# A decoder layer's first gate/up block, begun with two products on half of the tokens

## The chip, the cores and the metric

The kernel runs on one core of one Trainium2 chip. The metric is the device time of one execution in microseconds (us), taken as the median of several runs; the profile is of one execution of its own.

## What is computed

One layer of a post-norm decoder: 512 tokens, model width 2048, all in fp32. In the order of the work:

1. One projection of h feeds two token mixers: grouped attention in a sliding window of 128 with sinks, and causal differential attention. Both add a relative-position bias. They are gated, mixed and projected (W_o), then h = LN1(alpha*h + ...).
2. Cross attention into 256 memory rows (W_cq, W_kv, four heads, W_co), then h = LN2(alpha*h + ...).
3. The feed-forward part, with d_ff = 5632, then LN3:

```
g, u = split(h @ w_gate_up);  h = LN3(alpha*h + (silu(g) * u) @ w_down)
```

Each LN subtracts the mean, multiplies by the inverse standard deviation, then by a gain per column, and adds a bias per column.

## The kernel before

**Matmuls.** Every fp32 product is made of three fp32r products (`mm3`, L255 to L262): xh·wh, xh·wl and xl·wh, where `split` (L165) makes the parts: ACT casts h (L168), VectorE subtracts for l (L169). Tokens lie in four blocks t of 128. Weights come in chunks of 128x1024 (512 KB) over SyncE's queue (`dma`, L175); `dma_aside` (L178) is the software queue of POOL.

**The start.** POOL writes the bias rows to DRAM (rv_d), spreads them with three big transfers into rep_d, then copies the first keys (kd, eight transfers of 128 KB) and the first queries (q) into place; attention's first scores (L458) need those.

**W_co and LN2.** `gemm_n` (L277) makes W_co's four columns of 512; after each token block's matmuls `done` (L879) adds the residual (L880) and the statistics (L712). After column 3 `moments` (L714) makes mean and inverse deviation per token block, partly on POOL. `scale` (L724) normalises each of 16 tiles of 128x512 on ACT (L731) and multiplies by the gain's row on VectorE (L732).

**The gate/up products.** w_gate_up is taken in 11 blocks g of 512 gate and 512 up columns. Rows are cut in two halves, too, so a block has four quarters (11, 12, 21, 22), each of four chunks. Its result is made of seven products instead of eight, in Strassen's manner: each is a token operand (a11, s1, s2n, s4, s3, a12, a22) times a weight operand (11, t1, t2, 22, t3, 21, t4). The token operands cover 256 tokens and half of the columns: a11 and a12 are token blocks 0 and 1, a21 and a22 blocks 2 and 3, the others sums of them. The weight operands t1, t2 and t4 are sums of quarters that VectorE makes (L978 to L985).

`token_operands` (L917) runs ahead of all products, for all four parts j: it transposes z on TensorE (L928), evicts with the bias on ACT (L929), makes the sums on VectorE (L938 to L944) and splits all seven operands. `Quarters` (L949) loads the weights' chunks into the 13 buffers of the pool rp, makes operand chunks three ahead of their use and loads ten ahead. A product is 48 matmuls, 12 for each chunk. Results go to banks x, w and y; `each` (L1028) copies or adds them.

**Orders.** Only the loop over the sevens (L1098) has TensorE's order written by hand; elsewhere the compiler of the program orders each engine. In the last block, after product 2, `hidden` (L1066) reads five blocks of finished activations back (tiles araw, two of 512 KB each, from rp), waits for 6.0 us of matmul time to be issued and transposes them (L1076) between the matmuls, in that written order. rp's buffers are handed out in the program's order. W_down then runs in blocks of 5, 5 and 1; in the first, the bias row of LN2 is added to the residual (L1138), read back from z_d.

Of the kernel before, what the change touches and what calls it, by code (L numbers as in the profile page):

```python
# [128 lines left out]
def layer_kernel(ctx, tc, x, xT, memT, table, onehot, w_in, sinks, lams, subw, w_a, w_b, w_o,  # L129
# [272 lines left out]
    lt = cp.tile([P, 256], F32, name="lt")  # L402
# [293 lines left out]
    class Norm:  # L696
# [17 lines left out]
        def moments(self, t):  # L714

            mv = small(4, f"mv{t}")
            nc.vector.bn_aggr(mv[:, 0:2], self.st[t].rearrange("p c s -> p (c s)"))
            neg = small(1, f"neg{t}")
# [42 lines left out]
    z = [[None] * 4 for _ in range(NT)]  # L761
    ln1 = Norm(0, z)
    for c in range(4):
        for t in range(NT):
            z[t][c] = at(s="z", pool=zp)
            dma_aside(z[t][c], x[cols(t), c * 512 : (c + 1) * 512])
# [100 lines left out]
    for h in range(HC):  # L867
# [3 lines left out]
        oc.append((at(F32R, "och"), at(F32R, "ocl")))  # L871
        split(*oc[h], o_ps)

    ln1.add_bias()
    ln2 = Norm(1, z)
    for c in range(4):
        ln2.row(0, c, at(s="lnrow", pool=rows_pool))

        def done(t, ps, c=c):  # L879
            nc.vector.scalar_tensor_tensor(z[t][c], z[t][c], ALPHA, ps, ALU.mult, ALU.add)  # L880
            ln2.stats(t, c)
            if c == 3:
                ln2.moments(t)

        gemm_n(W_co, c, oc, done, tail=2)

# [3 lines left out]
    rp = open_pool("rp", 13, phase)  # L890

    def rt(s):
        return rp.tile([P, 1024], F32, tag="rp", name=nm(s))

# [5 lines left out]

    zs = z_tiles()
    for c in (0, 2, 1, 3):
        for t in range(NT):
            ln2.scale(t, c, zs[t][c])
    z = zs
    side.close()
    sp = open_pool("sp", 14, phase)
    gp = open_pool("gp", 6, side, side="right")

    def st(s, dt=F32R):  # L910
        return sp.tile([P, 2048], dt, tag="sp", name=nm(s))


    OPS = ("a11", "s1", "s2n", "s4", "s3", "a12", "a22")
    s_hl = {op: [st(op).rearrange("p (k q) -> p k q", k=HK) for _ in range(2)] for op in OPS}

    def token_operands(j):  # L917

        b = ln_gb[:, 2 * ln2.i + 1, :]
        halves = []  # L920
        for half in range(2):
            raw = rt("sraw")
            r4 = raw.rearrange("p (h k q) -> p h k q", h=2, k=2)
            for i in range(2):
                k = 2 * j + i + half * HK
                tp = bank("hT")
                for t in range(NT):
                    nc.tensor.transpose(tp[:, cols(t)], z[t][k // 4][:, cols(k % 4)], ident)  # L928
                nc.scalar.activation(r4[:, :, i, :], tp.rearrange("p (h q) -> p h q", h=2),  # L929
                                     AF.Identity, bias=b[:, k : k + 1])  # L930
            halves.append([raw[:, :512], raw[:, 512:]])
        (a11, a21), (a12, a22) = halves
        x, y = rt("ssum"), rt("ssum")
        s1, s2n, s4, s3 = x[:, :512], x[:, 512:], y[:, :512], y[:, 512:]
        made = {"a11": a11, "s1": s1, "s2n": s2n, "s4": s4, "s3": s3, "a12": a12, "a22": a22}
        for op in OPS:
            if op == "s1":
                nc.vector.tensor_sub(s1, a22, a21)  # L938
            elif op == "s2n":
                nc.vector.scalar_tensor_tensor(s2n, a11, -1.0, s1, ALU.mult, ALU.subtract)  # L940
            elif op == "s4":
                nc.vector.scalar_tensor_tensor(s4, s2n, -1.0, a12, ALU.mult, ALU.subtract)
            elif op == "s3":
                nc.vector.tensor_sub(s3, a11, a21)  # L944
            v = made[op].rearrange("p (k q) -> p k q", k=2)
            split(*(x[:, 2 * j : 2 * j + 2, :] for x in s_hl[op]), v)


    class Quarters:  # L949
# [4 lines left out]

        NEED = {"11": 0, "12": 1, "22": 2, "21": 5}

        def __init__(self):
            self.loads = [(28 * g + 4 * n + c, g, q, c) for g in range(NF)
                          for q, n in self.NEED.items() for c in range(4)]
            self.raw, self.parts, self.made, self.loaded = {}, [], 0, 0  # L960

        def load_to(self, n):
            while self.loaded < len(self.loads) and self.loads[self.loaded][0] < n:
                _, g, q, c = self.loads[self.loaded]
                i = 16 * g + 4 * list(QUARTERS).index(q) + c
                self.raw[g, q, c] = t = rt("r" + q)
                dma(t, w_gu[i * P * 1024 : (i + 1) * P * 1024].rearrange("(p f) -> p f", p=P))
                self.loaded += 1

        def make_to(self, n):  # L970
            while self.made < min(n, 28 * NF):
                g, i = divmod(self.made, 28)
                op, c = self.ORDER[i // 4], i % 4
                self.load_to(self.made + 1)
                r = {q: self.raw.get((g, q, c)) for q in QUARTERS}
                if op == "t1":
                    src = wst.tile([P, 1024], F32, tag="raw", name=nm("t1"))
                    nc.vector.tensor_add(src, r["11"], r["12"])  # L978
                elif op == "t2":
                    src = r["11"]  # L980
# [254 lines left out]
```

## Time and profile before

| what | us |
|---|---|
| median of 3 runs | 2751.59 (2750.56 to 2752.66) |
| the profiled execution | 2750.57 |
| its span, first to last instruction | 2748.8 |
| TensorE busy | 2691.0 (98%) |
| VectorE busy | 1544.7 (56%) |
| ACT busy | 1002.9 (36%) |
| POOL busy | 209.9 (8%) |
| mean granted TensorE clock | 0.991 |

The profile's times count from the span's first instruction; 1.8 us of the execution lie around the span. An arrow "x<-y" reads "x made from y"; "[0.73 <-DVE neg L719]" behind a row is the idle time before it and what ended it, and "issue" there means that the profile shows no wait for anything. In a timeline neighbouring instructions of one kind are merged (x15), and the end of one overlaps the start of the next. L-numbers are lines of the kernel before.

### The profile page before, as it was taken

To read this page: it belongs to the slowest core of one execution; us is meant where nothing else is said; L and a number is where in the kernel's file an instruction comes from. 1 tells how busy PE (TensorE), PEld (TensorE's weight loads), DVE (VectorE), ACT (ScalarE), POOL (GpSimd) and SP (SyncE) were. 2 spreads that over 40 slices of the span, in tenths; PEclk is the share of its full clock that TensorE was granted. 3 is DMA by queue.
4 is the path that set the end of the run, shared out by engine and by line. 5 is a ranking of instruction groups with operands and counts; after the bars stand their busy time and mean duration, and the time that the engine had idled before them with its cause. 6 is when DMAs were issued, how large, how long until landed. Compare 5 with 4: busy or idle time off the path is not lost.

```text
span 2748.8 us, 31093 instructions
## 1 busy us (share of the span) xinstructions
PE 2691.0 (98%) x12274; PEld 2221.4 (81%) x12274; DVE 1544.7 (56%) x2023; ACT 1002.9 (36%) x1424; POOL 209.9 (8%) x366
## 2 busy tenths in 40 slices
PE   8899999999999999999879999999999999999998
PEld 6788888888888888888768888888888878888886
DVE  4456545652333343365888888777777873233227
ACT  3344433442222232154454444444444451122112
POOL 2311212000000011000100000000000010000003
PEclk9999999999999999999989999999999999999999
DMA  8644636322222245333333334333233473343332
GB/s 276 151 113 105 146 113 145 100 84 93 99 93 100 93 136 170 93 114 118 115 128 115 117 136 138 138 130 123 100 130 120 139 269 101 93 137 99 101 95 105
DMA packets 107554, 341.64 MB, mean 124 GB/s; under 512 B 15071, under 2 KB 15631, under 8 KB 107408
## 3 DMA queue, kind: packets, MB, share of 16 engines
q1 hardware_dynamic: 81872, 277.91, 30.4%
q0 software_dynamic: 25536, 61.75, 8.7%
q8 instruction: 96, 1.57, 0.2%
q14 instruction: 50, 0.41, 0.0%
HBM read 301.79 MB, written 25.74 MB: 119 GB/s over the span
## 4 chain that ended last, share of the span: by engine, by line
PE 94%; DVE 2%; DMA 2%; issue 1%; ACT 1%; POOL 0%; POOLq 0%; DVEq 0%
PE ps L261 19%; PE ps L259 19%; PE ps L257 19%; PE y L257 4%; PE y L261 4%; PE y L259 4%; PE x L259 3%; PE x L261 3%; PE x L257 3%; PE w L257 3%; PE w L261 3%; PE w L259 3%; DMA kd<-kl 1%; PE o L543 1%; PE aT L1076 1%
## 5 line engine op out<-in xcount | busy, mean ns | idle before, releaser
L169 DVE TENSOR_TENSOR wl<-raw,wh 128x1024 fp32r<-128x1024 f32 (+1 forms) x313 | 379.4, 1213 | 804.5 <-ACT wh L168 803.7
L168 ACT CAST wh<-raw 128x1024 fp32r<-128x1024 f32 (+1 forms) x313 | 326.7, 1045 | 912.7 <-PE ps L261 495.1
L168 ACT CAST wh<-r 128x1024 fp32r<-128x1024 f32 x264 | 278.4, 1055 | 389.4 <-PE y L261 204.5
L169 DVE TENSOR_TENSOR wl<-r,wh 128x1024 fp32r<-128x1024 f32 x264 | 322.0, 1221 | 168.0 <-ACT wh L168 168.0
L257 PE MATMUL ps<-xh,wh 128*128 128x512 f32 x928 | 369.7, 399 | 6.8 <-ACT wh L168 4.5
L259 PE MATMUL ps<-xl,wh 128*128 128x512 f32 x928 | 369.4, 398 | 0.9 <-DVE xl L169 0.9
L261 PE MATMUL ps<-xh,wl 128*128 128x512 f32 x928 | 368.9, 398 | 0.0
L257 PE MATMUL ps<-wh,ah 128*128 128x512 f32 x656 | 258.4, 394 | 0.0
L261 PE MATMUL ps<-wh,al 128*128 128x512 f32 x656 | 258.1, 393 | 0.0
L259 PE MATMUL ps<-wl,ah 128*128 128x512 f32 x656 | 258.0, 393 | 0.0
L257 PEld LDWEIGHTS ps<-xh,wh 128*128 128x128 f32 x928 | 175.2, 189 | 45.8 <-ACT wh L168 4.5
L259 PEld LDWEIGHTS ps<-xl,wh 128*128 128x128 f32 x928 | 175.1, 189 | 39.7 <-DVE xl L169 1.8
L261 PEld LDWEIGHTS ps<-xh,wl 128*128 128x128 f32 x928 | 175.3, 189 | 37.6
L257 PE MATMUL x<-wh,a 128*128 128x512 f32 x352 | 140.4, 399 | 10.8 <-ACT sraw L929 5.8
L259 PE MATMUL x<-wl,a 128*128 128x512 f32 x352 | 140.0, 398 | 5.2 <-DVE wl L169 5.2
L257 PEld LDWEIGHTS ps<-wh,ah 128*128 128x128 f32 x656 | 123.2, 188 | 26.8
L261 PEld LDWEIGHTS ps<-wh,al 128*128 128x128 f32 x656 | 123.2, 188 | 26.5
L259 PEld LDWEIGHTS ps<-wl,ah 128*128 128x128 f32 x656 | 123.2, 188 | 26.3
L261 PE MATMUL x<-wh,a 128*128 128x512 f32 x352 | 139.5, 396 | 0.0
L261 PE MATMUL w<-wh,s 128*128 128x512 f32 x352 | 137.5, 391 | 0.0
L257 PE MATMUL w<-wh,s 128*128 128x512 f32 x352 | 137.5, 391 | 0.0
L259 PE MATMUL w<-wl,s 128*128 128x512 f32 x352 | 137.4, 390 | 0.0
(270 smaller groups left out, 4925.7 us busy)
## 6 DMA issues: line engine op xcount, KB each, us to landing
r<-in_w_gu SPq DMA_DIRECT2D x176, 512.0 KB, 3.3
raw<-in_w_in SPq DMA_DIRECT2D x131, 512.0 KB, 3.6
raw<-in_w_down SPq DMA_DIRECT2D x88, 512.0 KB, 3.5
raw<-in_w_o SPq DMA_DIRECT2D x32, 512.0 KB, 3.5
acts_d<-g POOLq DMA_DIRECT2D x44, 256.0 KB, 2.9
araw<-acts_d SPq DMA_DIRECT2D x22, 512.0 KB, 5.0
raw<-in_w_a SPq DMA_DIRECT2D x16, 512.0 KB, 3.4
raw<-in_w_b SPq DMA_DIRECT2D x16, 512.0 KB, 3.2
```

Source lines behind the costliest of these rows:

```text
L168: nc.scalar.copy(h, src)
L169: nc.vector.tensor_sub(l, src, f32(h))
L257: nc.tensor.matmul(ps, ah, bh, start=start, stop=False, **kw)
L259: nc.tensor.matmul(ps, ah, bl, start=False, stop=False, **kw)
L261: nc.tensor.matmul(ps, al, bh, start=False, stop=stop, **kw)
L543: nc.tensor.matmul(o4[i][:, :, dst, :], v[x][:, cols(kb)], p[y][:, :, src, :], start=first and m == 0, stop=last and m == 2, skip_group_ch ...
L1076: nc.tensor.transpose(tp[:, cols(t)], raw[t // 2][:, (t % 2) * 512 + i * P :][:, :P], ident)
```

## The change

- The order of VectorE and ACT is written by hand from W_co's last column to the first block's third product, and TensorE's from W_co's last column to the end of the sevens.
- The first block g = 0 has another order of products: 11 and 21 first. Both read only token blocks 0 and 1 (a11, a12) and add into the same bank x. `first_half(c)`, c = 0 to 7, makes their operands; the other five operands are made by functions that stand behind the matmuls of chunks 4 to 19 (list `after`), and the normalisation of the blocks stands in between.
- LN2's 16 tiles are normalised in place, without gain: two on ACT, 14 on VectorE (`normed`). Gain and bias of each column are applied when ACT evicts the transposes, 256 columns at a time. The residual gets gain and bias in W_down's first block, from row loads there.
- In block 0 the sums of weights come from accumulating transfers on POOL's queue, straight from DRAM: w22 onto the r12 chunks, w12 onto the r11 chunks after the split of 11. The quarters 12, 21 and 22 are therefore read a second time in this block. In the other blocks t1 is made in place in r11, and three of four chunks of 22 are loaded into buffers of the general weight pool.
- Memory: rp has 11 buffers instead of 13; operands lie in three kinds of buffers; tiles move between pools (also lt, LN3's rows, and mv and neg with two buffers). The oc splits stand behind `add_bias`. The scratch for the software queue's descriptors is 8192 instead of 4096.

The diff, cut to its core (removed functions are those of the kernel above):

```diff
--- the norm's tiles, the pools, W_co
-            mv = small(4, f"mv{t}")
+            mv = sm.tile([P, 4], F32, tag=f"mv{t}", bufs=2, name=nm("mv"))
...
-    act = open_pool("act1", 35, phase)
-    rows_pool = open_pool("rows", 4, side, side="right")
+    act = open_pool("act1", 39, phase)
...
-        oc.append((at(F32R, "och"), at(F32R, "ocl")))
-        split(*oc[h], o_ps)
+        oc.append(o_ps)
...
-        gemm_n(W_co, c, oc, done, tail=2)
...
-    rp = open_pool("rp", 13, phase)
+    rp = open_pool("rp", 11, phase)
+    gp = open_pool("gp", 6, phase)
+    sps = [open_pool("sp", 1, phase)]
...
--- token_operands (all seven operands ahead of the sevens) is removed; the quarters
+        FIRST = ("11", "21", "t1", "t2", "22", "t3", "t4")
         NEED = {"11": 0, "12": 1, "22": 2, "21": 5}
+        EARLY = {"11": 0, "12": 0, "22": 4, "21": 5}
...
+                if q == "22" and c < 3:
+                    t = wst.tile([P, 1024], F32, tag="raw", name=nm("raw"))
+                else:
+                    t = rt("r" + q)
...
+                if g == 0 and q == "12":
+                    self.add(t, "22", c)
...
+        def add(self, t, q, c):
+            nc.gpsimd.dma_start(t, self.src(0, q, c), accum_op=ALU.add)
...
+                if op == "21" and g == 0:
+                    src = wst.tile([P, 1024], F32, tag="raw", name=nm("raw"))
+                    dma(src, self.src(g, op, c))
+                elif op == "t1" and g:
+                    nc.vector.tensor_add(src, src, r["12"])
                 elif op == "t2":
-                    src = r["11"]
-                    nc.vector.tensor_add(r["12"], r["12"], r["22"])
-                    nc.vector.tensor_add(src, src, r["12"])
+                    if g:
+                        nc.vector.tensor_add(r["12"], r["12"], r["22"])
+                    nc.vector.tensor_add(src, src, r["22"])
...
                 split(*hl, src)
+                if g == 0 and op == "11":
+                    self.add(src, "12", c)
...
--- what makes the operands, and where it stands
+    def normed(t, c, aside=False):
+        mv, r = ln2.mv[t], z[t][c]
+        if aside:
+            nc.scalar.activation(r, r, AF.Identity, bias=mv[:, 3:4], scale=mv[:, 2:3])
+        else:
+            nc.vector.tensor_scalar(r, r, mv[:, 2:3], mv[:, 3:4], ALU.mult, ALU.add)
+        dma_aside(z_d[t][c], r)
+    def transposed(half, k0, dst, c):
+        tp = bank("hT")
...
+            nc.scalar.activation(o[:, q], tp[:, q], AF.Identity, bias=b_col[:, k : k + 1],
+                                 scale=g_col[:, k : k + 1])
+    def first_half(c):
+        op = ("a11", "a12")[c // 4]
+        transposed(0, 2 * c, op, c % 4)
+        op_split(op, c % 4)
+    def second_half(c):
+        transposed(1, HK + 2 * c, "a22", c)
+        transposed(1, 2 * c, "a21", c)
+        op_sum("s1", "a22", "a21", c)
+        op_split("s1", c)
+    def s3_s2n(c):
+        op_sum("a21", "a11", "a21", c)
+        op_sum("a11", "a11", "s1", c, True)
+        op_split("s2n", c, "a11")
+    def s4(c):
+        op_sum("a12", "a11", "a12", c, True)
+        op_split("s4", c, "a12")
...
+    for c in range(4):
+        for n, f in enumerate((second_half, s3_s2n, s4, lambda c: op_split("s3", c, "a21"),
+                               lambda c: op_split("a22", c))):
+            after[4 * n + 4 + c].append(lambda f=f, c=c: f(c))
+    after[0] = [lambda: first_half(2), lambda: first_half(3),
+                lambda: (normed(0, 2), normed(1, 2))]
+    after[1] = [lambda: first_half(4), lambda: first_half(5),
+                lambda: (normed(0, 3), normed(1, 3))]
+    after[2] = [lambda: first_half(6), lambda: first_half(7),
+                lambda: (normed(2, 2), normed(3, 2))]
+    after[3] = [lambda: (normed(2, 0), normed(3, 0)), lambda: (normed(2, 1), normed(3, 1))]
+    after[5].insert(0, lambda: (normed(2, 3), normed(3, 3)))
...
+    for c in range(4):
+        if c == 3:
+            PE_order.__enter__()
+            in_order.__enter__()
+        def done(t, ps, c=c):
+            if c == 3 and t == 1:
+                normed(0, 0, True)
+                normed(0, 1, True)
+            if c == 3 and t == 2:
+                first_half(0)
+            nc.vector.scalar_tensor_tensor(z[t][c], z[t][c], ALPHA, ps, ALU.mult, ALU.add)
+            ln2.stats(t, c)
+            if c == 3:
+                ln2.moments(t)
+            if c == 3 and t == 0:
+                quarters.make_to(1)
+            if c == 3 and t == 1:
+                normed(1, 0)
+                normed(1, 1)
+            if c == 3 and t == 2:
+                first_half(1)
+        gemm_n(W_co, c, oc, done, tail=2)
...
--- the sevens
+        for n, op in enumerate(quarters.ORDER if g else quarters.FIRST):
+            do(n, op)
+            if g == 0 and n == 2:
+                in_order.__exit__(None, None, None)
...
--- W_down's first block, and the program
-                    nc.vector.tensor_add(z[t][c], z[t][c], ln2.row(1, c))
+                    for i, f in enumerate((nc.vector.tensor_mul, nc.vector.tensor_add)):
+                        f(z[t][c], z[t][c], ln2.row(i, c, at(s="lnrow", pool=gp)
+                                                    if t == 0 else None))
...
-                   dynamic_dma_scratch_size=4096)
+                   dynamic_dma_scratch_size=8192)
```

## Rows read from the trace of the kernel before

**Rows 1.** The page: share of the chain that ended last, by engine.

```profile
PE 94%; DVE 2%; DMA 2%; issue 1%; ACT 1%; POOL 0%; POOLq 0%; DVEq 0%
```

**Rows 2.** TensorE's waits, whole run: us in total, times, longest.

```profile
PE s L458 <- DMA q<-ql: 9.8, 1, 9.8
PE hT L928 <- ACT sraw L929: 6.0, 2, 4.8
PE x L257 <- ACT sraw L929: 5.8, 1, 5.8
PE x L259 <- DVE wl L169: 5.2, 1, 5.2
```

**Rows 3.** Windows: length, busy us (instructions) per engine, TensorE's clock, DMA share, GB/s.

```profile
1360.00:1380.00 20.00, 8.76 (x40) 7.25 (x40) 18.28 (x29) 18.83 (x32) 5.40 (x11) 0.71 0.67 234
1380.00:1400.00 20.00, 8.99 (x20) 6.47 (x21) 20.00 (x31) 14.98 (x26) 0.00 (x0) 0.59 0.65 231
```

**Rows 4.** TensorE's timeline, 1352 to 1420: start, us, line, operation, tiles.

```profile
1353.49 0.40 PE L261 MATMUL ps<-wh,ocl 128*128 128x512 f32 x1
...
1354.73 2.15 PE L928 MATMUL hT<-ident,z 128*128 128x128 f32 x15 [0.73 <-DVE neg L719]
...
1380.80 0.80 PE L257 MATMUL x<-wh,a 128*128 128x512 f32 x1 [5.78 <-ACT sraw L929]
...
1407.77 0.39 PE L257 MATMUL w<-wh,s 128*128 128x512 f32 x1
...
1418.65 0.39 PE L257 MATMUL y<-wh,s2n 128*128 128x512 f32 x1
```

**Rows 5.** Groups by form: busy us, mean ns of one | idle before.

```profile
L731 ACT ACTIVATE z<-z,mv 128x512 f32<-128x512 f32 x48 | 35.5, 809 | 43.0 <-POOL mv L721 42.9
...
L605 DVE TENSOR_SCALAR pb<-pb,rb 128x512 f32<-128x512 f32 x8 | 3.9, 484 | 0.2
...
L837 ACT ACTIVATE pc<-sc,mc 128x256 f32<-128x256 f32 x16 | 7.4, 471 | 6.4 <-DVE mc L833 6.4
```

**Rows 6.** VectorE's timeline, 1343 to 1400.

```profile
1387.34 1.28 DVE L169 TENSOR_TENSOR a<-sraw,a 128x512 fp32r<-128x512 f32 x2
...
1395.77 3.49 DVE L169 TENSOR_TENSOR wl<-r,wh 128x1024 fp32r<-128x1024 f32 x3
```

**Rows 7.** The page: VectorE's busy tenths in 40 slices of the span.

```profile
DVE  4456545652333343365888888777777873233227
```

**Rows 8.** POOL's timeline, 10 to 95 us.

```profile
40.93 1.11 POOL L178 DMA_DIRECT2D rep_d<-rv_d  x1 [11.90 <-issue]
52.39 1.06 POOL L178 DMA_DIRECT2D rep_d<-rv_d  x1 [10.35 <-issue]
...
75.55 0.52 POOL L178 DMA_DIRECT2D kd<-kl  x1 [18.44 <-DMA rep_d<-rv_d]
```

**Rows 9.** The chain of waits, 60 to 95 us: start, us, what.

```profile
79.07 6.26 DMA q<-ql
```

**Rows 10.** DMA issues, 20 to 95 us, then the page's: KB each, us to landing.

```profile
rep_d<-rv_d POOLq DMA_DIRECT2D x1, 2560.0 KB, 22.9
rep_d<-rv_d POOLq DMA_DIRECT2D x1, 2304.0 KB, 11.2
...
araw<-acts_d SPq DMA_DIRECT2D x22, 512.0 KB, 5.0
```

**Rows 11.** Windows in the kernel's first 90 us.

```profile
30.00:45.00 15.00, 15.00 (x70) 12.41 (x69) 4.58 (x10) 3.96 (x7) 1.11 (x1) 1.00 0.53 166
84.00:87.00 3.00, 1.58 (x5) 1.42 (x6) 0.00 (x0) 0.00 (x0) 1.78 (x4) 0.50 0.65 134
```

**Rows 12.** Timelines of VectorE, SyncE's queue and TensorE, 2184 to 2225.

```profile
2189.69 1.22 DVE L169 TENSOR_TENSOR wl<-r,wh 128x1024 fp32r<-128x1024 f32 x1 [1.49 <-ACT wh L168]
...
2190.95 8.52 SPq L175 DMA_DIRECT2D araw<-acts_d  x4
...
2197.93 0.27 PE L1076 MATMUL aT<-ident,araw 128*128 128x128 f32 x1
```

More of the change, by code (lines that the diff above doesn't have):

```diff
@@ L917, in token_operands @@
[L917 to L946, printed above, removed]
@@ new lines, in rows, with op_split, op_sum @@
+    def rows(t, c):
+        return t[:, c * 512 : c * 512 + 512]
+    def op_split(op, c, raw=None):
+        for s in (op + "h", op + "l"):
+            if s not in ops:
+                ops[s] = st(s, kind="B" if op in ("s2n", "s4") else "R")
+        split(rows(ops[op + "h"], c), rows(ops[op + "l"], c), rows(raws[raw or op], c))
+    def op_sum(dst, a, b, c, neg=False):
+        o, a, b = (rows(raws[s], c) for s in (dst, a, b))
+        if neg:
+            nc.vector.scalar_tensor_tensor(o, a, -1.0, b, ALU.mult, ALU.subtract)
+        else:
+            nc.vector.tensor_sub(o, a, b)
@@ new lines, in layer_kernel @@
+    after = [[] for _ in range(28)]
+    for c in range(4):
[6 more added lines that the diff above has]
+                lambda: (normed(0, 3), normed(1, 3))]
@@ L1011, in layer_kernel, with product @@
     acts_d = [dr.tile([NT, P, 512], F32, name=nm("acts_d")) for _ in range(NF)]
+    OPS = {"11": "a11", "t1": "s1", "t2": "s2n", "22": "s4", "t3": "s3", "21": "a12", "t4": "a22"}
     def seven(g):
-        x, y, w = ([bank(s) for _ in range(2)] for s in "xyw")
-        def product(i, acc, first, last):
-            sh, sl = s_hl[OPS[i]]
+        acc = {}
+        made = {}
+        def product(n, op, s, first, last):
+            if s not in acc:
+                acc[s] = [bank(s) for _ in range(2)]
+            sh, sl = (ops[OPS[op] + i].rearrange("p (k q) -> p k q", k=HK) for i in "hl")
@@ L1064, in layer_kernel, with up @@
+        def up(t):
+            u2 = made["u2"]
+            nc.vector.tensor_mul(u2[t], u2[t], made["act"][t])
+            dma_aside(acts_d[g][t], u2[t])
+        for n, op in enumerate(quarters.ORDER if g else quarters.FIRST):
+            do(n, op)
+            if g == 0 and n == 2:
+                in_order.__exit__(None, None, None)
+            if g == NF - 1 and n == 2:
+                for j in range(FF_BLOCKS[0]):
+                    sides.add(hidden(j))
     hid = [[None] * 4 for _ in range(NF)]
@@ L1096, in __getitem__ @@
             return hid[self.g0 + k // 4][k % 4]
-    with tc.manual_schedule(engines={mybir.EngineType.PE}):
-        for g in range(NF):
-            if g == NF - 1:
-                feed.limit = len(feed.chunks)
-            seven(g)
-    side.close()
-    rows_pool = open_pool("rows2", 4, side, side="right")
+    for g in range(NF):
+        if g == NF - 1:
+            feed.limit = len(feed.chunks)
+        seven(g)
+    PE_order.__exit__(None, None, None)
     z = z_tiles()
@@ L1111, in layer_kernel @@
     ln2.rows, ln2.z = {}, z
-    for c in range(4):
-        ln2.row(1, c, at(s="lnrow", pool=rows_pool))
     ln3 = Norm(2, z)
```

165 lines of the change are left out of this document (94 added, 71 removed).

## The prediction

> **What bounds the kernel now.** I read the page's chain first [rows 1]: TensorE makes 94% of it, so only its holes, its slow clock and work added to it can move the time. The list of TensorE's waits over the whole run [rows 2] then says where the holes are: the longest single one is 9.8 us on a DMA into q, and the next three (6.0 in two pieces, 5.8, 5.2) all lie around the first gate/up block. [...] Fourth, TensorE's timeline there [rows 4]: the last W_co matmul starts at 1353.49; transposes stand in front of everything; the first product starts at 1380.80 with a matmul of 0.80 us (0.39 at full clock), and ends where w begins, 1407.77; the second ends where y begins, 1418.65. Those 10.88 us are the price of a product at full clock, 48 matmuls, and 2.72 us that of one of its four weight chunks.
>
> So the stage is bound by making operands for all seven products (28 casts, subtractions and sums on VectorE) ahead of the first.
>
> **The change, part by part. A, the gap.** The profiled run took 2750.57, 1.0 below the median of 2751.59; the sum is made against 2750.57.
>
> The new first two products read only token blocks 0 and 1. Bound: W_co ends at 1353.7, 64 transposes at 0.13 us (15 in 2.15 us, less the 0.28 of the last one's own length [rows 4]) are 8.5, two products 21.8: product two could end at 1384.0, not 1418.65. At most 34.6 us are to be had, and none would be if the order by hand kept every wait.
>
> What is taken off: 16 normalisations on ACT at 0.81 ([rows 5], L731) and VectorE's 16 gain multiplications no longer precede the transposes. What comes: 14 normalisations on VectorE (nearest row the 128x512 scale of L605, 0.48; I use 0.40 from start to start, since successive ones overlap by some 0.08 as those of [rows 6] do) and 2 on ACT; 32 evictions of 256 columns on ACT, each as L837 (0.47), or 15 us, for 16 of 512, on an engine that the normalisations have left.
>
> First half, from these durations in the written order. Waits of TensorE: about 1.1 for the normalised block 1 (its moments go through POOL), 0.8 for the second chunk's subtraction, 0.6 and 1.4 for transposes behind VectorE's normalisations, 1.4 between the products, since both write bank x and ACT must copy it out first. Together 5.3: product two ends at 1389.3.
>
> Then t1 and t2. VectorE (its order written out to the end of t1, and little to choose from in t2) does per chunk: a weight subtraction (three in a row take 3.49, so 1.14 each from start to start), two operand sums and one subtraction at 0.60 (two take 1.28 [rows 6]), and an estimated 0.7 of waiting for ACT's cast: 3.6 against TensorE's 2.72. With t2's sum of weights (one more 1.14) it is 4.8; once s4 takes the place of s3 and s2n, 4.2. Two chunks lose 0.9, two 2.1, two 1.5, two 0.3, which is 9.6, with some 1.4 of backlog 11.0. The sums of weights that went to accumulating DMAs are what keeps it from another four times 1.14. Product four ends at 1389.3 + 21.8 + 11.0 = 1422.1, before 1418.65 + 21.77 = 1440.4: 18.3 gained. After it VectorE has caught up. **A = -18** (-12 to -25: evictions 0.1 slower and normalisations at 0.6 cost 4; both faster, and the operand chain hidden better, give 5).
>
> [...]
>
> **What moves elsewhere.** POOL's queue gets eight accumulating transfers. The four r12 += w22 stand first, each behind its r12 load, and behind them wait the moments' small POOL operations, the z_d stores and the four r11 += w12. The r12 loads go out while W_co still runs, so 0 is taken, with up to 5 if they are late. The 6 MB loaded a second time are 26 us at the 234 GB/s of [rows 3], in a stretch in which DMA is 0.67 and 0.65 busy at present: 0, by the slack of some 27 us that the slower rival works out. Gain and bias of the residual move into W_down's first block, 16 VectorE multiplications of some 0.7 where VectorE is 2 to 3 tenths busy (the last quarter of [rows 7]), and 8 row loads for 4. The oc splits now stand behind add_bias in the program; W_co's first columns are ordered automatically: 0 to 3, taken as 0.
>
> **B, the ring.** The scratch of the software queue is doubled for the whole program. POOL issues three big rep_d transfers; the second and third go out at 40.93 and 52.39, after idles of 11.90 and 10.35 marked "issue", that is with no semaphore to wait for [rows 8]. The landings (11.2 us for the second, 22.9 for the third [rows 10]) show that what follows goes out just as the one before has landed: 52.39 is 11.46 after 40.93, and the eighth kd transfer, after 18.44 of idle, at 75.55, 23.16 after 52.39. q follows it: issued 79.07, landing 6.26 later at 85.33, TensorE idle for 9.8 since 75.6 [rows 2, 9], and after it at half clock (0.50 from 84 to 87 [rows 11]). I read the idles as descriptors that don't fit. With room for all, the last kd goes out with its neighbours instead of some 3 us after them, and the rep_d transfers overlap from 30 to 45, where DMA is 0.53 busy ([rows 11]: 7 of 15 us are free). q lands about 10 to 11 earlier, near 75, before TensorE runs dry: the idle goes, and with it some of the slow clock. **B = -10.5** (0, if the idles aren't the ring, to -11.5).
>
> **C, the last block.** The pool rp shrinks from 13 to 11 buffers. In the last block hidden() needs two for its araw loads while four r11, four r12, one r22 and two r21 are held: eleven. Before, the first araw issues at 2190.95, as VectorE ends a split begun at 2189.69 [rows 12]. After, the first load takes the buffer of r22's last chunk, freed by the split two chunks (5.44) on, 2196.4, and the second that of r12's first, one chunk later, 2199.1. A load takes 5.0 [rows 10], and the transposes are fixed in TensorE's order at 2197.93: it waits for the first until 2201.4, 3.5, and for the second until 2204.1, 5.5 in all if loads take 5.0, 3.5 if they take 3 us as lighter ones do; I take 4.5. The next hidden blocks find the pool just as full: I take one product chunk, 2.7, for the second, hidden in part behind the first's delay, and 2 for the fourth, which needs four buffers where three are free. Behind each such wait stands all of TensorE's order. **C = +9** (+2, if buffers come free sooner than I count, to +12.5).
>
> Sum: 2750.57 - 18 - 10.5 + 9 = **2731**.
>
> **The rivals.** *The ring is not it.* For it: nothing in the trace names descriptors. Against: every idle ends with a landing. Time 2731 + 10.5 = 2741.5; chance 0.18.
>
> *Better than that:* VectorE's chain hides and the last block's loads find buffers in time: A -23, C +3, 2720; for it, VectorE's work up to t2's last split adds up to 56 us (16 weight subtractions and 4 sums at 1.14, 14 normalisations at 0.40, 34 operand sums and subtractions at 0.60, some 7 for the block sums), which ends near 1402 if begun 8 ahead of W_co's end; against, it is serial with ACT in each chunk. Chance 0.13.
>
> *The wait only moves.* A hand order can stall both engines behind one late item, and TensorE's clock falls in such holes: here it fell, with TensorE busy less than half of the time [rows 3]. At half clock a chunk costs up to 2.72 more; seven of the sixteen so, 19, eat A: 2731 + 19 = 2750; chance 0.13, a third of it still below the 0.2% line.
>
> *Slower.* The four accumulating transfers r11 += w12, on POOL's queue, are issued from about 1352 to 1364, each after its chunk's split; t1's last chunk wants them at about 1391. If they run one behind the other at T each, the last lands at 1352 + 4T. As the plain loads of 512 KB take 5.0 [rows 10], T of 5.0 lands it at 1372, no loss. The sum loses its whole gain, and 0.2% of the time more, when the last is 26 us late, T = 16; at T = 18 it is 33 late, 2764. No row shows an accumulating transfer, so 0.07. [...]
>
> **How the numbers follow.** 0.2%, 5.5 us, is about what a measurement of this kernel can tell from no change: below 2746 is faster, above 2757 slower. Forecast 0.49, the ring 0.18, better 0.13, the wait moves 0.13, slower 0.07. Faster: 0.49 + 0.18 + 0.13 + 0.05 = 0.85; same 0.08; slower 0.07. Range: low, A -25, B -11.5, C +2: 2716. High, A -12, B 0, C +9: 2747.
>
> **What would show it.** A: the first x matmul near 1358 instead of 1380.80, the second product's end near 1389, full clock throughout, waits of TensorE on VectorE's wl, 1 to 2 us each, in t1 and t2. B: the rep_d issues one behind the other, no q wait in TensorE's list. C: the first araw issued 5 us later against its chunk, TensorE waiting at L1076's transposes. Wrong: a first product that starts after 1370, a rep_d idle that stays, t1's casts waiting for a DMA, or waits in the last block above 12 us.

## The result, and the profile after

The changed kernel takes 2773.58 us (median of 4 runs, 2772.12 to 2774.37) against 2751.07 for the kernel before in the same runs: a ratio of 1.0081, with an interval of 1.0063 to 1.0098. It is 22.5 us slower where 2731, 20 us faster, was forecast, and lies 27 us above the range.

The page of the changed kernel shows little; TensorE's share of the chain is that of [rows 1]:

```profile
PE 94%; DVE 2%; DMA 2%; ACT 1%; issue 1%; POOL 0%; SPq 0%; ACTq 0%; POOLq 0%; DVEq 0%
```

Its list of TensorE's waits over the whole run answers to [rows 2]. The q wait of 9.8 us and the waits for sraw are gone; in their place stand waits for read-back activations (aT), for VectorE's split of oc, for ACT's vch, and a row of small ones on VectorE and ACT:

```profile
PE aT L1197 <- DMA araw<-acts_d: 9.7, 5, 2.5
PE ps L261 <- DVE oc L169: 9.0, 1, 9.0
PE oc L257 <- ACT vch L168: 5.2, 1, 5.2
PE hT L1020 <- DVE z L1011: 4.6, 3, 3.1
...
PE y L257 <- ACT wh L168: 4.1, 2, 3.0
PE ps L259 <- DVE wl L169: 3.1, 3, 1.0
...
PE w L257 <- ACT wh L168: 2.5, 1, 2.5
PE aT L1197 <- DVE al L169: 2.5, 1, 2.5
```

Where time came from and went is seen best by milestones, TensorE's first matmul of a stage in either timeline (us; "end" is the first matmul of what follows, and the operands' transposes stand ahead of W_co's last twelve matmuls in the kernel after):

| milestone | before | after | after less before |
|---|---|---|---|
| last matmul of the memory's kv | 1304.22 | 1293.95 | -10.3 |
| first of W_co | 1310.20 | 1307.12 | -3.1 |
| first transpose for the block's operands | 1353.73 | 1363.19 | +9.5 |
| end of the block's second product | 1418.65 | 1403.75 | -14.9 |
| end of its fourth | 1440.41 | 1443.01 | +2.6 |
| first of the next block | 1473.05 | 1476.31 | +3.3 |
| first of W_down | 2245.41 | 2259.66 | +14.3 |
| last of W_down | 2735.42 | 2756.79 | +21.4 |
| span | 2748.8 | 2771.8 | +23.0 |

So six stretches have to be explained: a gain at the start; a loss of 19.8 us in and around W_co; a gain of 24.4 from the transposes to the end of the second product; a loss of 17.5 us in the third and fourth; losses in the last block (11.0) and in W_down (7.1).

POOL's timeline, to be held against [rows 8]: the three rep_d transfers go out in one piece.

```profile
28.64 3.33 POOL L178 DMA_DIRECT2D rep_d<-rv_d  x3 [3.84 <-DMA rv_d<-rv]
...
65.23 0.51 POOL L178 DMA_DIRECT2D kd<-kl  x1 [16.27 <-DMA rep_d<-rv_d]
```

VectorE's timeline at W_co: 16 additions of add_bias, and only then the four subtractions of oc, the first of which W_co's third matmul needs. TensorE's timeline under it: it starts W_co, stops after two matmuls for 8.97 us, and goes on at about half clock (0.51 granted from 1316.6 to 1321.0):

```profile
1306.32 9.72 DVE L754 TENSOR_TENSOR z<-z,lnrow 128x512 f32<-128x512 f32 x16 [3.04 <-DMA lnrow<-in_lns]
1315.96 2.47 DVE L169 TENSOR_TENSOR oc<-oc,oc 128x512 fp32r<-128x512 f32 x4
```

```profile
1307.34 0.39 PE L259 MATMUL ps<-wl,oc 128*128 128x512 f32 x1
1316.69 0.80 PE L261 MATMUL ps<-wh,oc 128*128 128x512 f32 x1 [8.97 <-DVE oc L169]
```

The windows over the first block (columns as in [rows 3]). TensorE is no longer half idle. But VectorE, called the bound in the prediction, is busy only 14 of 20 us in the first three. In the fourth it is full, at 19.64, and there TensorE is busy least, 13.43, with its clock at 0.83:

```profile
1360.00:1380.00 20.00, 15.69 (x79) 12.40 (x78) 14.28 (x27) 11.74 (x19) 12.01 (x18) 1.00 0.41 99
1380.00:1400.00 20.00, 17.00 (x89) 13.59 (x87) 13.95 (x21) 14.67 (x27) 6.13 (x11) 1.00 0.92 278
1400.00:1420.00 20.00, 16.01 (x67) 12.15 (x66) 13.50 (x17) 12.63 (x20) 0.11 (x1) 0.91 0.11 45
1420.00:1440.00 20.00, 13.43 (x42) 9.62 (x41) 19.64 (x24) 9.19 (x13) 0.00 (x0) 0.83 0.15 53
```

The last block, in the timelines of SyncE's queue and of TensorE (compare [rows 12]): the loads are issued at 2199.65, that is 5.4 later than before, beyond the shift of 3.3; four waits of TensorE follow, of which these are the first and the last:

```profile
2199.65 13.49 SPq L175 DMA_DIRECT2D araw<-acts_d  x4
```

```profile
2203.67 0.33 PE L1197 MATMUL aT<-ident,araw 128*128 128x128 f32 x1 [2.32 <-DMA araw<-acts_d]
...
2218.18 0.33 PE L1197 MATMUL aT<-ident,araw 128*128 128x128 f32 x1 [2.35 <-DMA araw<-acts_d]
```

In W_down's first block VectorE stands for a row load, with the subtraction al, which TensorE's transposes wait for (2.46 us, at 2274.85), behind it. VectorE's timeline, then POOL's: the row loads go out behind the stores of the last block's results, which free their buffers.

```profile
2269.45 1.22 DVE L169 TENSOR_TENSOR wl<-raw,wh 128x1024 fp32r<-128x1024 f32 x1
2272.90 1.29 DVE L1256 TENSOR_TENSOR z<-z,lnrow 128x512 f32<-128x512 f32 x2 [2.24 <-DMA lnrow<-in_lns]
2274.11 0.68 DVE L169 TENSOR_TENSOR al<-aT,ah 128x512 fp32r<-128x512 f32 x1
```

```profile
2270.67 1.70 POOL L178 DMA_DIRECT2D lnrow<-in_lns  x3 [1.51 <-DMA acts_d<-g]
```

### The profile page after: what moved, and what is told of

Its sections match the earlier page's. It is cut to its first block, busy times and chain, and to the rows that moved or that the text cites. A ratio compares the mean times of both kernels' runs of the same rounds, so it can differ in the third digit from the quotient of the medians.

```text
span 2771.8 us, 31144 instructions
## 1 busy us (share of the span) xinstructions
PE 2700.4 (97%) x12274; PEld 2223.1 (80%) x12274; DVE 1546.3 (56%) x2029; ACT 998.5 (36%) x1426; POOL 219.4 (8%) x374
## 4 chain that ended last, share of the span: by engine, by line
PE 94%; DVE 2%; DMA 2%; ACT 1%; issue 1%; POOL 0%; SPq 0%; ACTq 0%; POOLq 0%; DVEq 0%
PE ps L259 20%; PE ps L261 20%; PE ps L257 19%; PE y L261 4%; PE y L259 4%; PE y L257 4%; PE w L261 3%; PE w L257 3%; PE w L259 3%; PE x L257 3%; PE x L261 3%; PE x L259 3%; PE aT L1197 1%; PE o L543 1%; PE o L627 1%; DMA araw<-acts_d 1%
## 5 line engine op out<-in xcount | busy, mean ns | idle before, releaser
L169 DVE TENSOR_TENSOR wl<-raw,wh 128x1024 fp32r<-128x1024 f32 (+1 forms) x350 | 424.5, 1214 | 823.1 <-ACT wh L168 822.3
L168 ACT CAST wh<-raw 128x1024 fp32r<-128x1024 f32 (+1 forms) x350 | 365.7, 1045 | 974.9 <-PE ps L261 508.0
L168 ACT CAST wh<-r 128x1024 fp32r<-128x1024 f32 x271 | 285.3, 1054 | 386.1 <-PE y L261 122.6
L169 DVE TENSOR_TENSOR wl<-r,wh 128x1024 fp32r<-128x1024 f32 x271 | 330.6, 1220 | 138.7 <-ACT wh L168 138.6
L261 PE MATMUL ps<-oh,wl 128*128 128x512 f32 x256 | 100.6, 393 | 0.0
L259 PE MATMUL ps<-ol,wh 128*128 128x512 f32 x256 | 100.4, 392 | 0.0
L257 PE MATMUL ps<-oh,wh 128*128 128x512 f32 x256 | 100.2, 393 | 0.0
L257 PE MATMUL ps<-wh,mixh 128*128 128x512 f32 x256 | 99.6, 389 | 0.0
L259 PE MATMUL ps<-wl,mixh 128*128 128x512 f32 x256 | 99.6, 389 | 0.0
L261 PE MATMUL ps<-wh,mixl 128*128 128x512 f32 x256 | 99.6, 389 | 0.0
```

Of the source, the lines that this page charges most:

```text
L168: nc.scalar.copy(h, src)
L169: nc.vector.tensor_sub(l, src, f32(h))
L257: nc.tensor.matmul(ps, ah, bh, start=start, stop=False, **kw)
L259: nc.tensor.matmul(ps, ah, bl, start=False, stop=False, **kw)
L261: nc.tensor.matmul(ps, al, bh, start=False, stop=stop, **kw)
```

## The experiments

All times are medians, beside the kernel before on the same chip; "against before" is the difference from it there. The changed kernel stands at +22.5, and an edit's worth is the distance from that. Its ratio has an interval of 1.0063 to 1.0098, so a worth below some 5 us (e4, e7, e9, e10, e15) isn't told from nothing by the times alone.

**e1: oc's splits ahead of add_bias.**

```diff
-    ln1.add_bias()
     phase.close()
...
         oc[h] = hl
+    for c in range(4):
+        ln1.row(1, c, at(s="lnrow", pool=gp))
+    ln1.add_bias()
```

> The changed kernel, with the four oc splits ahead of add_bias in VectorE's order (add_bias moved behind them, its rows in gp buffers). Theory (the sum's missing term is the stage of W_co: TensorE stands 9.0 us for VectorE's oc split, which is queued behind 16 additions of add_bias, and then runs some 4 us at half clock): the 9.0 us wait goes, W_co ends 10 to 12 us earlier, 2773.6 - 11 = 2762 (2759 to 2766). Rival (the wait only moves: W_co's first residual additions then stand behind add_bias, or the first block's chain of operands starts no earlier): 2771 or more, with a new wait of TensorE in W_co or ahead of the first product.

Measured: 2762.97, +13.0 against before (ratio 1.0046, 1.0031 to 1.0061): worth 9.6. The wait of 9.0 is not in TensorE's list any more, and the block's fourth product ends at 1433.07, 9.9 earlier than in the changed kernel. The order of two steps in the program, costed at nothing, is worth nearly half of the 22.5. The 5.2 on vch stays (5.5).

**e2 and e3: the ring alone**, back at 4096 in the changed kernel, and raised in the kernel before.

```diff
-                   dynamic_dma_scratch_size=8192)
+                   dynamic_dma_scratch_size=4096)
```

> The changed kernel with the software queue's scratch back at 4096 and nothing else. Theory (the ring holds up the rep_d transfers): the idles marked issue ahead of the second and third rep_d come back, q is late again, TensorE waits about 9.8 us near 85 us; everything up to the memory attention is 10.3 us later, 2773.6 + 10 = 2784 (2778 to 2785; less than 10 if the late W_co loads, 5.2, are met by the later start). Rival (the gain at the start comes from something else in the change): no difference, 2773.

Measured: 2782.44, +32.4 (1.0119, 1.0104 to 1.0134): 9.9 lost; POOL's idles of 12.11 and 10.80 marked "issue" are back, and TensorE's wait for q of 10.0.

```diff
-                   dynamic_dma_scratch_size=4096)
+                   dynamic_dma_scratch_size=6656)
```

> The kernel before with the scratch at 6656 (8192 does not fit beside its pools) and nothing else. Theory (ring): rep_d issues close together, the q wait of 9.8 us gone or small, 2751.1 - 10.3 = 2741 (2739 to 2745). If two rep_d transfers fit but not three: about half of it, 2746. Rival (the ring is not it): 2751.

Measured: 2739.32, -10.7 (0.996, 0.9946 to 0.9974). In POOL's timeline of e3 the three go out together, and no q wait is left:

```profile
28.85 3.33 POOL L178 DMA_DIRECT2D rep_d<-rv_d  x3 [4.15 <-DMA rv_d<-rv]
```

The size of the forecast's part B is shown both ways.

**e4: the first loads later.**

```diff
-    quarters.load_to(4)
...
     for c in range(4):
+        if c == 2:
+            quarters.load_to(4)
         if c == 3:
             PE_order.__enter__()
```

> The changed kernel with the first eight quarter loads and the four accumulating transfers r12 += w22 emitted inside W_co, ahead of its third column, not ahead of W_co. Theory (these 6 MB stand in front of and beside the W_co loads, whose late casts hold up vch and the oc products: a wait of 5.2 us and some 2 us of slow clock): oc starts 5 us earlier, but the oc splits still wait behind add_bias, which waits for its rows: 2773.6 - 4 = 2769 (2764 to 2773). Rival (the loads are needed that early: t1 or t3 then wait for r11 or r12): 2775 or more, with waits of ACT's weight casts on a DMA in the first block.

Measured: 2771.66, +21.6 (1.0076, 1.0061 to 1.0091). It settles nothing: SyncE's queue issues the loads of r from 1263 to 1299 as in the changed kernel (1265 to 1301), so the compiler of the program put these loads where they had stood, though their line had moved.

**e9, e7 and e10: the accumulating transfers.** e9 holds r12's loads back by a dependency, e7 has VectorE make all sums, e10 only r12's.

```diff
-        EARLY = {"11": 0, "12": 0, "22": 4, "21": 5}
+        EARLY = {"11": 0, "12": 1, "22": 4, "21": 5}
...
+                if g == 0 and q == "12":
+                    nc.vector.memset(t[:, :1], 0.0)
                 dma(t, self.src(g, q, c))
```

> The changed kernel with the four loads of r12 in the first block, and so the four accumulating transfers onto them, held back until the first products run: VectorE writes one column of each r12 buffer, in its written order, before the load. Theory (these 4 MB, sent off while the memory attention still runs, hold up the W_co loads, whose casts stand ahead of vch on ACT, and add_bias's row loads behind them on POOL's queue): the wait of 5.2 us ahead of the oc products and the slow clock after it go, add_bias starts earlier too: 2773.6 - 7 = 2767 (2763 to 2770). Rival (the r11 loads on SyncE's own queue are enough to delay W_co's): 2771 or more. Rival (r12 then comes too late for t3): a wait in the first block's later products, 2774 or more.

Measured: 2771.74, +22.2 (1.008, 1.0065 to 1.0095): worth 0.3. The wait on vch is gone and W_co starts at 1299.15, 8.0 earlier. But the second product ends at 1403.37 (1403.75): the accumulating transfers now run beside the loads of 21, and a transpose waits 5.7 for VectorE, which stands 6.6 for ACT's cast of a weight chunk, and ACT 6.3 for that chunk's load. Between 1365 and 1400 the accumulating transfers land after 13.8 there, and the plain loads beside them after 13.5 to 18.0 (medians).

```diff
-                elif op == "t1" and g:
+                elif op == "t1":
...
-                    if g:
-                        nc.vector.tensor_add(r["12"], r["12"], r["22"])
+                    nc.vector.tensor_add(r["12"], r["12"], r["22"])
...
-                if g == 0 and q == "12":
-                    self.add(t, "22", c)
...
-                if g == 0 and op == "11":
-                    self.add(src, "12", c)
```

> The changed kernel with the first block's sums of weights made by VectorE, as in the other blocks, and no accumulating transfers. Two theories of their worth. If VectorE is the bound in t1 and t2: eight additions of 1.14 come back there, 9 us, and the W_co loads, no longer beside the accumulating transfers, save up to 7 (the 5.2 us wait ahead of the oc products and 2 of half clock): 2776 (2771 to 2780). If the accumulating transfers cost more than they save: 2767 or less, and t1 and t2 not longer than now (39.3 us together).

Measured: 2772.72, +23.2 (1.0085, 1.0068 to 1.0102): no difference. W_co starts 7.7 earlier, the second product ends at 1394.9, 8.9 earlier, and t1 and t2 take 48.6 in place of 39.3: the transfers save 9.3 there and cost 8.9 ahead of it, for the same total.

```diff
-                if g == 0 and q == "12":
-                    self.add(t, "22", c)
...
+                elif op == "t3" and g == 0:
+                    nc.vector.tensor_add(src, src, r["22"])
```

> The changed kernel without the four accumulating transfers onto r12: VectorE adds w22 to r12 when t3's weights are made, three products later; the four onto r11 stay. Theory (these transfers, which run while the memory attention ends, hold up the W_co loads, and moved in between the first products they hold up others): W_co starts 8 us earlier, t1 and t2 stay as they are, and four additions of 1.14 vanish beside the fourth product: 2773.6 - 8 = 2766 (2763 to 2769). Rival (VectorE has no room beside the fourth and fifth product, or the chunks of 22, held until t3, keep others from their buffers): 2771 or more, with waits on VectorE's wl in those products.

Measured: 2770.03, +19.7 (1.0071, 1.0056 to 1.0085): worth 2.8, less than expected and not clear of noise. W_co starts 5.7 earlier and t1 and t2 end at 1437.6, 5.4 earlier.

**e5: the last block's transposes later.**

```diff
-        yield 6.0
+        yield 6.0 if g >= FF_BLOCKS[0] else 10.0
```

> The changed kernel with the transposes of the five blocks read back in the last gate/up block written 10.0 us of matmul time behind their loads, not 6.0. Theory (these loads find rp's eleven buffers taken and come 5.4 us later, while the transposes stand where they stood): TensorE's four waits on araw (2.3, 1.4, 1.1, 2.4) and some 4 us of half clock behind them go, the last blocks' transposes move on into W_down: 2773.6 - 9 = 2765 (2761 to 2768). Rival (what is put off there is only paid in W_down): 2771 to 2775.

Measured: 2760.27, +10.7 (1.004, 1.0025 to 1.0055): worth 11.8. The four waits are gone and W_down starts 14.8 earlier; a wait of 4.8 for araw there gives some of it back. A larger rp, the buffers themselves, was not tried.

**e6: gain and bias on POOL in W_down.**

```diff
-                    for i, f in enumerate((nc.vector.tensor_mul, nc.vector.tensor_add)):
+                    for i, f in enumerate((nc.gpsimd.tensor_mul, nc.gpsimd.tensor_add)):
```

> The changed kernel with the multiplication by LN2's gain row and the addition of its bias row, in W_down's first block, done by POOL and not by VectorE. Theory (VectorE stands still there for row loads that wait for gp buffers, and the subtraction al, queued behind it, holds up TensorE's transposes): the waits near 2275 and 2280 (2.5 and 2.6) and the half clock after them go: 2773.6 - 7 = 2767 (2765 to 2770). Rival (W_down is late because its activations are read back late after the last block): no difference, 2772 or more.

Measured: 2766.24, +16.7 (1.0058, 1.0043 to 1.0073): worth 5.8. W_down starts at 2259.05, 0.6 earlier than without the edit, and ends 6.7 earlier: it takes 491.0 us, not 497.1 (490.0 in the kernel before). Its loss came from the row loads on VectorE, not from the last block.

**e11, e14 and e15: who writes the order.** e11 leaves VectorE's and ACT's order to the compiler, e14 only VectorE's, e15 only ACT's.

```diff
-    in_order = tc.manual_schedule(engines={mybir.EngineType.DVE, mybir.EngineType.Activation})
...
-            in_order.__enter__()
...
-            if g == 0 and n == 2:
-                in_order.__exit__(None, None, None)
```

> The changed kernel with VectorE's and ACT's order left to the compiler of the program from W_co's last column on; TensorE's stays written. Theory (the written order of these two isn't what costs; the loss lies ahead of it, in W_co, and behind it, in the last block and W_down): not faster, 2773 to 2790, since the chain for the first two products then has rivals on both engines. Rival (the written order makes the two engines wait for each other, so that the wait only moved): 2765 or less, with t1 and t2 together under 35 us (39.3 now).

Measured: 2751.08, +0.8 (1.0001, 0.9992 to 1.001): worth 21.7, the largest single effect, and against the theory stated. In the windows of e11 VectorE is busy 17, 17 and 20 of 20 us where it was 14, and TensorE hardly stops:

```profile
1360.00:1380.00 20.00, 18.48 (x92) 15.26 (x91) 16.86 (x30) 17.88 (x32) 12.66 (x19) 0.95 0.75 198
1380.00:1400.00 20.00, 19.84 (x104) 16.41 (x102) 17.21 (x23) 17.28 (x30) 0.00 (x0) 1.00 0.37 144
1400.00:1420.00 20.00, 18.05 (x78) 14.49 (x79) 20.00 (x26) 13.62 (x19) 0.00 (x0) 1.00 0.11 32
```

The second product ends 9.8 us earlier than in the changed kernel, and the third and fourth take 24.7 us there (1393.91 to 1418.63) and not 39.3. W_co's three waits of about 1.05 vanish too; two of them lie in columns ahead of the written stretch, the third at its start, and why the first two go is not shown. VectorE is busy for all of those 24.7 us: its work is still the limit of the two products there. In the changed kernel it has 32.8 us of work between the same two points, since it did less ahead of them, and stands idle for 6.4 more. What it does in the written order is seen in its timeline of the changed kernel: in the second product it stands 0.9 to 1.2 us for ACT's cast of one operand, and later for ACT's evictions, with normalisations ready behind it:

```profile
1380.70 0.69 DVE L169 TENSOR_TENSOR a12l<-raw,a12h 128x512 fp32r<-128x512 f32 x1 [1.21 <-ACT a12h L168]
1382.27 0.69 DVE L169 TENSOR_TENSOR a12l<-raw,a12h 128x512 fp32r<-128x512 f32 x1 [0.88 <-ACT a12h L168]
...
1394.72 0.69 DVE L999 TENSOR_TENSOR raw<-raw,raw 128x512 f32<-128x512 f32 x1 [1.23 <-ACT raw L1025]
1396.10 0.69 DVE L169 TENSOR_TENSOR s1l<-raw,s1h 128x512 fp32r<-128x512 f32 x1 [0.69 <-ACT s1h L168]
...
1412.12 1.22 DVE L169 TENSOR_TENSOR wl<-r,wh 128x1024 fp32r<-128x1024 f32 x1 [2.63 <-ACT wh L168]
```

The longest stand is the last row. ACT's timeline shows what ran ahead of the cast that ends it: the SiLU of the finished x, with the load of its table. TensorE waits 2.48 us for that cast, too; no run moved the SiLU alone.

```profile
1408.78 1.28 ACT L1159 ACT_TABLE_LOAD   x1
1410.07 1.07 ACT L1159 ACTIVATE x<-x 128x512 f32<-128x512 f32 x2
1411.04 1.05 ACT L168 CAST wh<-r 128x1024 fp32r<-128x1024 f32 x1
```

```diff
-    in_order = tc.manual_schedule(engines={mybir.EngineType.DVE, mybir.EngineType.Activation})
+    in_order = tc.manual_schedule(engines={mybir.EngineType.Activation})
```

> The changed kernel with ACT's order written and VectorE's left to the compiler. If the loss is VectorE's (it stands for ACT's casts and evictions with other work behind it): most of the 22 us come back, 2753 to 2760. If it is ACT's (the weight casts stand behind operand casts that wait for VectorE): 2768 or more. If either order alone is enough to lock the two together: both this and the other one 2765 or more.

Measured: 2757.53, +7.7 (1.0028, 1.0017 to 1.0039): worth 14.9.

```diff
-    in_order = tc.manual_schedule(engines={mybir.EngineType.DVE, mybir.EngineType.Activation})
+    in_order = tc.manual_schedule(engines={mybir.EngineType.DVE})
```

> The changed kernel with VectorE's order written and ACT's left to the compiler. If the loss is VectorE's: 2768 or more. If it is ACT's: 2753 to 2760. If either order alone locks the two together: 2765 or more.

Measured: 2768.94, +19.1 (1.0071, 1.0058 to 1.0084): worth 3.4. VectorE's order is the one that costs most. Freeing ACT's alone gives 3.4, which is not clear of noise; once VectorE's is free, freeing ACT's too gives the remaining 6.8.

**e12, e13, e16 and e17: the edits together.** e12 has those of e1, e10, e5 and e6; e13 that of e11 besides; e16 is e13 without e10's; e17 is e13 without e6's.

> The changed kernel with four edits together: the oc splits ahead of add_bias, VectorE's sum for r12 in place of the accumulating transfers, the last block's transposes 10.0 behind their loads, LN2's gain and bias on POOL in W_down. Theory (the losses lie at four separate places, so they add): 2773.6 - 11 - 8 - 12 - 6 = 2737 (2732 to 2744), below the kernel before. Rival (they overlap, each wait hiding another): 2745 to 2755.

Measured: 2752.76, +2.5 (0.9997, 0.998 to 1.0014), but from 2739.33 to 2760.11 in 12 runs. The lowest agrees with the sum, the median doesn't.

> The changed kernel with the four edits of e12 and, as fifth, VectorE's and ACT's order left to the compiler. Theory (the written order costs 22 us by itself, in the first block and in W_co, apart from the other four places): 2741, the lower of the times that e12 showed, less 22: 2719 (2714 to 2726). Rival (the written order and the other four overlap): 2735 or more. If the times scatter over 15 us again, as e12's did, the scatter is not of the written order.

Measured: 2722.20, -27.7 (0.9918, 0.9896 to 0.994), the fastest here; four of six runs within 2 us, two at 2738 and 2739.

> As e13, but with the accumulating transfers onto r12 kept. Theory (they delay the W_co loads, and so the oc products, by 5 us and some 2 of slow clock): 2719 + 6 = 2725 (2720 to 2731), oc with a wait of some 5 us on ACT's vch. Rival (with the oc splits early this wait is covered): the same as e13. It also tells whether the scatter of e12 comes with the r12 edit.

Measured: 2733.39, -16.5 (0.9931, 0.9912 to 0.9951), again scattered (2721.3 to 2738.1), with the wait on vch (5.4) back. The scatter isn't e10's nor the written order's; with e13 and e16 scattered over 17 to 19 us, what e10's edit is worth there stays open. In e13's profile VectorE's subtraction of weights, 1.22 us elsewhere, takes 11.31 once in W_down, while POOL works through its row operations; VectorE's timeline, then POOL's:

```profile
2240.07 11.31 DVE L169 TENSOR_TENSOR wl<-raw,wh 128x1024 fp32r<-128x1024 f32 x1 [1.04 <-ACT wh L168]
2251.31 0.68 DVE L169 TENSOR_TENSOR al<-aT,ah 128x512 fp32r<-128x512 f32 x1
```

```profile
2239.34 5.02 POOL L1252 TENSOR_TENSOR z<-z,lnrow 128x512 f32<-128x512 f32 x4
2244.32 0.57 POOL L178 DMA_DIRECT2D lnrow<-in_lns  x1
2244.91 5.01 POOL L1252 TENSOR_TENSOR z<-z,lnrow 128x512 f32<-128x512 f32 x4
```

> As e13, but with LN2's gain and bias rows back on VectorE: four edits (oc splits ahead of add_bias, r12 summed by VectorE, transposes 10.0 behind their loads, VectorE's and ACT's order left to the compiler). In e13's profile weight subtractions of VectorE that take 1.22 alone take up to 11.3 beside POOL's row operations. Theory (the scatter of e12, e13 and e16 is of these: how often VectorE's subtraction loses to POOL differs from run to run): no scatter, all runs within 4 us, and subtractions in W_down of 1.2 throughout; 2721 + 3, since with the transposes later and the other edits the row loads' wait costs less than the 7 it cost in the changed kernel: 2724 (2719 to 2729). Rival (the scatter comes with the shifted start of W_down, or with the r12 edit): lowest and highest run over 10 us apart again.

Measured: 2730.01, -20.6 (0.9926, 0.9913 to 0.994), 2728.65 to 2730.63: no scatter. It is 6 above the value expected; a wait of 5.5 for araw is left in W_down, where e13's profile has 0.3. The subtractions there (groups by form, 2200 to 2300) are back at their length:

```profile
L169 DVE TENSOR_TENSOR wl<-raw,wh 128x1024 fp32r<-128x1024 f32 x16 | 19.6, 1224 | 34.0 <-ACT wh L168 34.0
```

So taking e6's edit out ends the scatter. That the lengthened subtractions make it isn't shown: e6 alone has one of 8.78, and its four runs lie within 3.3 us; the profiles of e12 and e13, both of runs near the lowest (2741.71 and 2720.82), have one of 10.56 and the one of 11.31. What such a subtraction can cost is seen in e16's profile, of a run of 2730.55: it takes 16.24 there, and TensorE waits 6.3 for it. No trace here is of a run near the highest of e12 or e13.

The single gains add up: 9.6 + 21.7 + 11.8 + 2.8 = 45.9, less the 22.5 of the changed kernel, gives -23.4 for e17; -20.6 was measured. Of that the ring is -10.7 (e3), so what is left of the change, restructured so, is worth some 10 us, if the two add.

## Why the prediction was wrong

**B, the ring: right in size and in place.** -10.5 forecast, -10.3 at the kv milestone, -10.7 in e3. One step of it did not come: "the last kd goes out with its neighbours". The last three kd copies still stand 2.9, 5.3 and 16.3 us behind landings of rep_d; the gain is that the three rep_d transfers run together.

**C, the last block: right in mechanism, close in size.** The first load was put at 2196.4; with the shift of 3.3 that is 2199.7, and it came at 2199.65. The waits add up to 7.1, where 9.2 were counted (4.5, 2.7 and 2), and the stretch loses 11.0, with the slow clock behind them (0.52 granted from 2206 to 2212, 0.58 from 2218 to 2222), which the sum left out: that the two are so near is in part luck. The range took C at 9 at its upper end, though C's own bound was +12.5; this would not have reached 2773.

**A failed, at three steps.** It was -18 and turned into +13.6 between the kv milestone (-10.3) and the block's end (+3.3). Most of the miss lies ahead of the products: 22.5 us (19.8 up to the first transpose, and W_co's last twelve matmuls, 2.7, behind it) where 0 was taken: waits of 9.0, 5.2 and three of about 1.05, and the slow clock behind the first two (0.51 and 0.52 granted). The first half itself came close, with 7.1 of waits for 5.3; the largest was 3.06 for block 1's normalisation, put at 1.1. Its sign of being wrong, a first product after 1370, showed: 1370.08.

1. "The oc splits now stand behind add_bias in the program; W_co's first columns are ordered automatically: 0 to 3, taken as 0." The compiler kept the program's order: 9.0 of wait, worth 9.6 (e1). The bound was there to be computed: the same 16 additions took 9.71 in the kernel before, behind the oc splits, and W_co's first matmul followed oc's without a gap.
2. "The r12 loads go out while W_co still runs, so 0 is taken, with up to 5 if they are late." They went out while the memory attention still ran (the loads of r start at 1265), and with the transfers added onto them they made others late: W_co's loads land after 9.9 (4.1 before), and 5.2 of wait and a slow clock follow (0.52 granted from 1299.5 to 1304.0). e7 and e9 show 8 us at W_co's start. As tried here, it is no net loss: whoever makes these sums pays about as much elsewhere (e7, e9, e10).
3. "VectorE (its order written out to the end of t1, and little to choose from in t2) does per chunk ... 11.0." TensorE's waits in the two products came to 10.6, near the 11.0 by luck: one of 2.48 stands behind ACT's SiLU, which the chain per chunk doesn't have, and 6.6 come after 1420, where VectorE is full with what it had not done before. The 6.9 that the same matmuls took longer, most of it at half clock (0.50 granted from 1413.4 to 1416.0, 0.53 from 1426.5 to 1430.0, 0.54 from 1433.3 to 1436.7), was left out (39.3 measured for the two products, 32.8 forecast). The chain per chunk was taken as given, and so was the work left for VectorE at the start of t1. Both came from the written order: with the same operations and no written order the two products take 24.7 (e11). The prediction had a figure on the other side, 56 us of VectorE's work ending near 1402, and gave it 0.13.

**What moves elsewhere** was the fourth step, taken as 0 in the words "16 VectorE multiplications of some 0.7 where VectorE is 2 to 3 tenths busy, and 8 row loads for 4". Counted as busy time this is right. But the row loads need buffers that come free at the last block's end, and VectorE stood for them, with work behind it that TensorE needed: 7.1 in W_down, 5.8 of it shown by e6.

**The rivals.** "The wait only moves" named the mechanism ("a hand order can stall both engines behind one late item") at 2750; the written order was the largest single part (21.7, e11) and had companions that no rival named: oc's splits (9.6, e1) and the rows in W_down (5.8, e6). The slower rival did not happen: accumulating transfers of 512 KB landed after 6.1 (onto r11, 1355 to 1420) and 8.8 (onto r12), where 16 was the point from which it decides; only in e9, among many loads, did they come near it (13.8). The plain loads beside the two kinds took 4.7 and 5.7, so an accumulating transfer took 1.3 and 1.5 times as long as a plain load. The normalisation on VectorE took 0.54 (0.46 from start to start, where the sum had 0.40).

## What to carry to other kernels

A written order is a claim about every wait in it. Where two engines hand work back and forth, as VectorE and ACT do here, each can stand for the other with ready work behind it, so cost the order by the idle time that it makes, not by busy time. A step that is moved is costed against what now stands ahead of it on its engine, even where a compiler orders the engine. Loads that can go early may do so in front of somebody else's (W_co's landed after 9.9 and not 4.1). A pool made smaller, or a tile lent from another pool, sets the earliest time of a load: look who waits in order behind the buffer.

## What the runs showed of the hardware

While POOL works, a subtraction on VectorE can take many times its length: one of two 128x1024 operands in SBUF, 1.22 us alone, took 11.31 in e13 while POOL did eight operations of about 1.25 us on SBUF, and 16.24 in e16 beside twelve; both ended 1.1 to 1.5 us after the last of these. With POOL's operations moved to VectorE (e17) the weight subtractions from 2200 to 2300 took 1.22 and 1.23 on average (wl<-raw and wl<-r). Why the subtraction takes so long is not shown; it lasted through eight and twelve of POOL's operations in a row, not through one.

The software queue's scratch (`dynamic_dma_scratch_size`) sets how many of the rep_d transfers can be under way: at 4096 one at a time, with idles on POOL that no semaphore explains (11.90 and 10.35 in the kernel before, 12.11 and 10.80 in e2); at 6656 (e3) and 8192 (the changed kernel) all three, issued together in 3.33 us.
